# Layer 1's values and gates: where the stage's buffers lie, when its first loads go out, and the order of its tiles

## The chip, the core and the metric

The kernel runs on one core of one Trainium2 chip. A core has five engines that work from queues of their own: TensorE (PE in the profile; its weight loads are PEld), VectorE (DVE), ScalarE (ACT), GpSimd (POOL) and SyncE (SP), which here only issues DMAs. Each engine takes its instructions in a fixed order and waits on semaphores, so an instruction that waits holds up all that stand behind it on its engine. The metric is the device time of one execution in microseconds (us); less is better. SBUF is the on-chip memory with 128 partitions, PSUM the banks into which TensorE writes.

## The reference

Two layers over 2048 latent tokens and 256 context tokens of width 1024. The second, odd layer is the one that matters here. It multiplies the normalized tokens by one wide weight matrix and gets queries, keys, values and gates; queries and keys are normalized per head. Each token, on a grid of 32 rows by 64 columns, attends to a window of 8 by 16 neighbours with a bias per offset, and to all context tokens:

```python
q, k, v, z = jnp.split(u, 4, axis=-1)
...
s_lat = s_lat + bias.astype(jnp.float32)[None]
s_lat = jnp.where(col_mask[None, None, :, None, :], s_lat, -jnp.inf)
s_ctx = jnp.einsum('bqhd,bchd->bhqc', qr, k_ctx, preferred_element_type=jnp.float32) * scale
p = jax.nn.softmax(jnp.concatenate([s_lat, s_ctx], axis=-1), axis=-1)
...
y = jnp.dot(o.reshape(...) * jax.nn.silu(z_x), w_out)
x = x + gate * y
```

All is float32. The kernel makes a product of that precision from three matmuls: each operand is split into a high and a low part, and high x high, high x low and low x high are summed.

## The kernel before

Tokens come in 18 tiles of 128: tiles 0 and 1 are context, 2 to 17 latent. The odd layer's weights come in 8 groups of 512 columns, called j: 0 and 1 are queries, 2 and 3 keys, 4 and 5 values, 6 and 7 gates. A *cell* (t, j) is the product of tile t with group j: 8 steps of three 512-column matmuls. A gate cell takes two tiles at once and has 16 steps of six 256-column matmuls, in two halves with a PSUM bank each.

**`odd_qk`** makes queries and keys, and at its end also some of values and gates. Its last cells are, for tiles 16 and 17, groups 0 to 3, then the gate cell with group 6, then (16, 4) and (17, 4). Its pool `osA` holds, in the order of first use: the gains, two squares (2 KB per partition each), four small sums, four outputs `onat` (2 KB), two high and two low query tiles `oqh`, `oql` (2 KB) and four key tiles `okt` (8 KB). Key tiles, values and gates are stored to memory by DMAs that GpSimd issues (L1394, L1428, L1433).

**`odd_vz`** makes the rest of values and gates, and beside it, per head, each query's largest score (`maxes`), which attention needs. `weave` interleaves the two: after each step of a product come 0.57 steps of row maxima on average, and a product may run at most 15 steps of maxima ahead. One step of maxima is two matmuls, scores against the context keys (L1500) and against the window's keys (L1507). VectorE reduces them; for the window it adds the head's table first (L1513). The table is a bias (L1484, loaded) to which GpSimd adds two masks (L1485, L1486). ScalarE copies the head's queries into a half-zeroed tile `mz` (L106 from `by_tile`); VectorE zeroes the other halves once (L1467). Loads of the mask, queries, keys and tables are issued by SyncE, later queries by ScalarE.

A tile's cells need its high and low parts. There is room for two tiles; when a tile's last cell is done, `reload` brings the tile after next: load `x` (L376), ScalarE's copy to the high part, VectorE's subtraction for the low part (L380). A gate runs through ScalarE's tanh and VectorE's product (L1415) into a value buffer `ovz`; the bank comes free after that. There are two banks for products and six for the maxima.

The pools of `odd_vz` (`osB`, `omB`) lie over `osA`. A new tile waits for the last use of each old tile under it, among them DMAs that still store it.

**`odd_attention`** begins when the products end. Its loads are chained in one order on SyncE (`load`, L111). Its pools lie over the weights and pools of the stages before: query tiles, the first two tables and the first mask over the weights of groups 6 and 7, the key chunks over those of group 6. It starts with two steps against context keys, then takes window steps, whose scores get a masked table on VectorE (L1773); the products with the values follow some steps later (L1624, L1642).

The order of instructions on each engine is set by a planner that runs through the program with times of its own and gives each engine the instruction that is ready first, older ones ahead.

Of the kernel before, what the change touches and what calls it, by code (L numbers as in the profile page):

```python
# [17 lines left out]
P = 128  # L18
# [70 lines left out]
class Kern:  # L89
# [282 lines left out]
    def reload(self, l, t):  # L372

        nc, sp = self.nc, self.prp
        x = self.tl(sp, [P, D], "x", bufs=1)
        nc.sync.dma_start(x[:], self.H[l, t])  # L376
        h = x[:].rearrange("p (k t) -> p k t", k=KD)
        hi, lo = self.slots(t)
        self.act(hi, h)
        nc.vector.tensor_tensor(out=lo, in0=h, in1=hi, op=ALU.subtract)  # L380
        return hi, lo
# [910 lines left out]
    def odd_qk(self, ws, win, hT):  # L1292
# [7 lines left out]
        with ExitStack() as es:  # L1300
# [101 lines left out]
            for j in (0, 1, 2, 3, 6, 4):  # L1402
                cells += [((NT - 2, NT - 1), j)] if j == 6 else [(t, j) for t in (NT - 2, NT - 1)]
# [31 lines left out]
    def odd_vz(self, ws, win, hT):  # L1435
# [3 lines left out]
        with ExitStack() as es:  # L1439
            sp = self.pool(es, "osB", bufs=2, side="left", reuse_waits="tile")  # L1440
            mp = self.pool(es, "omB", bufs=2, side="left", reuse_waits="tile")
            pp = self.pool(es, "opB", bufs=2, space=PSUM, reuse_waits="tile")
            mk = self.tl(mp, [P, NR + NC], "maskq", bufs=1)
            nc.sync.dma_start(mk[:], self.i["maskq"])

            def cell(t, j):
                wh, wl = win[j]
                w = lambda k: wh[:, k, :], lambda k: wl[k][:]
                if j > 5:
                    for b in (0, 2):  # L1450
                        ps = self.tl(pp, [P, 512], "gm")
                        yield from self.pair_steps(ps, b, w)
                        n = self.tl(sp, [P, 512], "ovz", bufs=3)
                        self.gate(n, ps[:])
                        self.store_z(t, (j - 6) * 4 + b, n)
# [4 lines left out]
                n = self.tl(sp, [P, 512], "ovz", bufs=3)  # L1460
# [3 lines left out]
            zq = [[self.tl(mp, [P, 512], f"mz{i}{a}", F32R, bufs=1) for a in range(2)] for i in range(2)]  # L1464
            for i in range(2):
                for z in zq[i]:
                    nc.vector.memset(z[64 - i * 64 : 128 - i * 64].bitcast(F32), 0.0)  # L1467

            def queries(n, eng):
                h, g = divmod(n, 4)  # L1470
                b = (h % 2) * 64
                q = self.tl(mp, [P, 512], "mq", F32R, bufs=1)
# [3 lines left out]
            def maxes():  # L1476
                post, q = None, queries(0, nc.sync)
                for h in range(16):
                    j, b = h // 2, (h % 2) * 64
                    if b == 0:  # L1480
                        k = self.tl(mp, [P, T], "mk", F32R, bufs=2)
                        nc.sync.dma_start(k[:].bitcast(F32), self.K1[j])
                    tb = self.tl(mp, [P, NR, NC], "mtab", bufs=2)
                    nc.sync.dma_start(tb[:], self.i["rpb_q"][h].rearrange("p (r c) -> p r c", r=NR))  # L1484
                    nc.gpsimd.tensor_tensor(out=tb[:], in0=tb[:], in1=mk[:, :NR].unsqueeze(2).to_broadcast([P, NR, NC]), op=ALU.add)  # L1485
                    nc.gpsimd.tensor_tensor(out=tb[:], in0=tb[:], in1=mk[:, NR:].unsqueeze(1).to_broadcast([P, NR, NC]), op=ALU.add)  # L1486
                    m = self.tl(mp, [P, 16, 5], "mm")
                    nc.vector.memset(m[:], -3e38)
                    kl = k[:, CTX:].rearrange("d (r c) -> d r c", r=32)
                    for R in range(16):  # L1490
                        g, c = divmod(R, 4)
                        if c == 0:
                            zt = zq[h % 2][g % 2]
# [28 lines left out]
                    def post(h=h, mc=mc):  # L1522
                        pt = self.tl(pp, [P, 512], "mx", bufs=6)
                        nc.tensor.transpose(pt[:16, :P], mc[:], self.ident[:])
                        r = self.tl(mp, [P, P], "mr", F32R, bufs=1)
# [7 lines left out]
            cells = [((NT - 1, NT - 2), 7), (NT - 1, 5), (NT - 2, 5)]  # L1533
            for t in range(NT - 4, 0, -2):
                cells += [(t + 1, 4), (t + 1, 5), ((t, t + 1), 6), ((t, t + 1), 7), (t, 4), (t, 5)]
            cells += [(t, j) for j in (4, 5) for t in (1, 0)]
            gemms = self.stream(cells, hT, cell, lambda t: self.reload(1, t))
# [3 lines left out]
    def odd_attention(self, out, right, left, wout):  # L1541
# [4 lines left out]
        with ExitStack() as es:  # L1546
# [26 lines left out]
            for x in ones["kc"] + ones["kt"]:  # L1573
                nc.gpsimd.memset(x[64:65].bitcast(F32), 1.0)
# [12 lines left out]
            def values(j):  # L1587
                V = self.tl(vp[j % 2], [P, NT, P], "ov", bufs=1)
# [14 lines left out]
            def mask(tabs, mk):  # L1603
                for tb in tabs:
                    nc.gpsimd.tensor_tensor(out=tb[:], in0=tb[:], in1=mk, op=ALU.add)
# [95 lines left out]
            mask(tabs[0], load_mask(first.rearrange("p (r c) -> p r c", r=NR)))  # L1701
            kt.append(chunk(0, 0))
            V[0] = values(0)
            kt.append(chunk(0, 1))
            values_ctx(0, V[0])
# [241 lines left out]
```

## Time and profile before

| | us |
|---|---|
| median of 3 runs | 3570.43 |
| lowest, highest | 3565.54, 3573.92 |
| the profiled execution | 3572.7 |
| its span | 3570.9 |

| engine | busy us | share |
|---|---|---|
| TensorE matmul | 3492.2 | 98% |
| VectorE | 2384.3 | 67% |
| ScalarE | 1403.2 | 39% |
| GpSimd | 1221.3 | 34% |

The stage in question lies between about 2550 and 2995 us of the span; attention follows. A row of a timeline reads: start, length, engine, line, operation, out<-in, shape, count, and in brackets how long the engine stood idle before it and what ended that. A row of waits reads: who waited for whom, total us, times, longest. The chain is the work that ended last, followed back from the end. L106 and L111 are helpers that record many different instructions; there the tile's name tells which it is.

### The profile page before, as it was taken

The page shows a single profiled execution, that of the slowest core. Times are in us where ns is not written, and L with a number is a line of the kernel's source. Part 1 is how long each engine was busy: PE and PEld are TensorE (multiplying, and loading weights), DVE is VectorE, ACT ScalarE, POOL GpSimd, SP SyncE. Part 2 cuts the span into 40 slices and gives each one's busy share as a digit, 9 for nine tenths or more (in the row PEclk, how much of TensorE's full clock was granted, in tenths as well). Part 3 has the DMA queues.
Part 4 walks back from the last instruction along what each step waited for, and adds up shares of the span by engine and source line. Part 5 has one row for each costly group of instructions (what it writes and reads, how often), then busy time and mean ns, then how long its engine had stood idle before and what let it go on. Part 6 is the DMA issues. An engine that isn't in the chain of part 4 may idle for free.

```text
span 3570.9 us, 53484 instructions
## 1 busy us (share of the span) xinstructions
PE 3492.2 (98%) x19260; PEld 2758.9 (77%) x19260; DVE 2384.3 (67%) x5020; ACT 1403.2 (39%) x2656; POOL 1221.3 (34%) x1363
## 2 busy tenths in 40 slices
PE   8999999999999999999999999999999999999899
PEld 6888999999996666665667878888798997555577
DVE  4677767888886777798764344544688883777721
ACT  4545551111116555555553124444422223555510
POOL 1443430101011222212312233333454544777744
PEclk9999999999999999999999999999999999999999
DMA  7555554222243343424534554556744338887654
GB/s 254 150 148 168 146 173 125 87 77 87 68 120 86 81 110 83 108 76 125 155 112 145 162 168 122 148 150 174 227 149 153 118 125 222 218 216 212 181 179 148
DMA packets 386914, 513.75 MB, mean 144 GB/s; under 512 B 61229, under 2 KB 264061, under 8 KB 380746
## 3 DMA queue, kind: packets, MB, share of 16 engines
q1 hardware_dynamic: 353242, 418.68, 40.4%
q0 software_dynamic: 21888, 62.56, 5.9%
q10 hardware_dynamic: 11520, 29.09, 2.4%
q8 instruction: 153, 2.51, 0.3%
q14 instruction: 111, 0.91, 0.1%
HBM read 330.61 MB, written 179.59 MB: 143 GB/s over the span
## 4 chain that ended last, share of the span: by engine, by line
PE 85%; DVE 6%; DMA 4%; ACT 2%; issue 2%; POOL 2%; SPq 0%; POOLq 0%; DVEq 0%; ACTq 0%
PE gm L131 8%; PE gm L129 8%; PE gm L130 8%; PE av L1008 6%; PE mx L707 4%; PE st L1066 4%; PE st L1067 3%; PE st L1068 3%; PE gm L190 3%; PE gm L191 3%; PE gm L192 3%; PE o L1642 2%; PE st L1612 2%; PE st L129 2%; PE o L1624 2%; PE st L130 2%
## 5 line engine op out<-in xcount | busy, mean ns | idle before, releaser
L1057 DVE TENSOR_TENSOR acc<-acc,apt 128x512 f32<-128x512 f32 x512 | 380.7, 775 | 141.9 <-ACT apt L106 139.2
L708 DVE TENSOR_REDUCE mm<-mx 128x1 f32<-128x512 f32 (+1 forms) x656 | 391.0, 628 | 86.2 <-PE mx L707 78.9
L106 ACT ACTIVATE apt<-st 128x512 f32<-128x512 f32 (+1 forms) x592 | 345.5, 595 | 243.8 <-PE st L1068 204.6
L1008 PE MATMUL av<-apt,av 128*64 128x512 f32 (+1 forms) x1184 | 270.0, 592 | 0.0
L1066 PE MATMUL st<-aq,akh 97*128 97x512 f32 x576 | 245.5, 426 | 0.6 <-ACT apt L106 0.2
L707 PE MATMUL mx<-mk,mq 96*128 96x512 f32 (+1 forms) x656 | 241.7, 371 | 0.0
L106 ACT ACTIVATE u<-gm 128x352 f32<-128x352 f32 (+1 forms) x144 | 70.5, 497 | 428.4 <-PE gm L131 182.6
L1067 PE MATMUL st<-aq,akh 96*128 96x512 f32 x576 | 228.1, 396 | 0.0
L1068 PE MATMUL st<-aq,akl 96*128 96x512 f32 x576 | 227.9, 396 | 0.0
L106 ACT ACTIVATE opt<-opt 128x930 f32<-128x930 f32 (+9 forms) x144 | 119.5, 830 | 231.7 <-POOL opt L1813 139.6
L1513 DVE CUSTOM_DVE_ANT_1 mx<-mx,mtab 128x465 f32<-128x465 f32 (+12 forms) x576 | 180.1, 342 | 31.4 <-PE mx L1507 25.9
L1008 PEld LDWEIGHTS av<-apt,av 128*64 128x64 f32 x1184 | 80.1, 136 | 152.7 <-issue 150.1
L1773 DVE TENSOR_TENSOR opt<-st,tab 128x64 f32<-128x64 f32 (+10 forms) x576 | 142.9, 314 | 72.3 <-PE st L1613 39.3
L1648 POOL TENSOR_TENSOR oacc<-oacc,opt 128x682 f32<-128x682 f32 (+9 forms) x144 | 173.2, 1224 | 31.9 <-ACT opt L106 30.6
L1066 PEld LDWEIGHTS st<-aq,akh 97*128 97x128 f32 x576 | 108.3, 188 | 72.5 <-issue 42.1
L1068 PEld LDWEIGHTS st<-aq,akl 96*128 96x128 f32 x576 | 109.5, 190 | 25.2
L707 PEld LDWEIGHTS mx<-mk,mq 96*128 96x128 f32 x656 | 123.3, 188 | 6.0
L1067 PEld LDWEIGHTS st<-aq,akh 96*128 96x128 f32 x576 | 109.9, 191 | 16.9
L106 ACT ACTIVATE x<-px,modB,modA 128x128 f32<-128x128 f32 x272 | 99.3, 469 | 59.3 <-PE px L355 49.6
L131 PE MATMUL gm<-w0h,hlo 128*128 128x512 f32 x288 | 114.1, 396 | 5.4 <-DVE hlo L380 5.4
L1612 PE MATMUL st<-q,kt 128*128 128x480 f32 (+5 forms) x256 | 98.8, 388 | 20.4 <-DVE opt L1773 15.3
L129 PE MATMUL gm<-w1h,hhi 128*128 128x512 f32 x288 | 115.1, 400 | 2.9 <-DVE ovz L1415 2.9
(594 smaller groups left out, 10288.1 us busy)
## 6 DMA issues: line engine op xcount, KB each, us to landing
q<-Q SPq DMA_DIRECT2D x48, 512.0 KB
H<-x ACTq DMA_DIRECT2D x36, 512.0 KB
adaw<-ada_w SPq DMA_DIRECT2D x64, 256.0 KB
x<-H SPq DMA_DIRECT2D x32, 512.0 KB
K1t<-okt POOLq DMA_DIRECT2D x32, 512.0 KB, 6.8
kt<-K1t SPq DMA_DIRECT2D x32, 512.0 KB
mtab<-rpb_q SPq DMA_DIRECT2D x16, 899.0 KB
QT<-qkhl SPq DMA_DIRECT2D x36, 384.0 KB
```

The source lines that it names most:

```text
L106: return self.nc.scalar.activation(out, in_, func, **kw)
L129: self.nc.tensor.matmul(out, lh(k), rh(k), start=j == 0, stop=False)
L130: self.nc.tensor.matmul(out, lh(k), rl(k), start=False, stop=False)
L131: yield self.nc.tensor.matmul(out, ll(k), rh(k), start=False, stop=j == n - 1)
L707: mm = nc.tensor.matmul(ps[:, :w], q[:A_QK, (t % 6) * P : (t % 6) * P + P], k[:A_QK, k0 : k0 + w], start=True, stop=True)
L708: nc.vector.tensor_reduce(out=m[:, t, n : n + 1], in_=ps[:, :w], axis=AX.X, op=ALU.max)
L1008: nc.tensor.matmul(O[j, nb][i * 64 : i * 64 + 64, :w], V[j, kt // TT][:, kt % TT, i * 64 : i * 64 + 64], pts[i][:, :w], start=n == 0, stop ...
L1057: self.add = nc.vector.tensor_tensor(out=acc[i][:, :w], in0=a[:, :w], in1=pts[i][:, :w], op=ALU.add)
L1066: nc.tensor.matmul(ps[:, :w], kh[: A_QK + 1, i, kq], qh[: A_QK + 1, :w], start=True, stop=False)
L1067: nc.tensor.matmul(ps[:, :w], kh[:A_QK, i, kq], ql[:A_QK, :w], start=False, stop=False)
L1068: mm = nc.tensor.matmul(ps[:, :w], kl[:A_QK, i, kq], qh[:A_QK, :w], start=False, stop=True)
L1513: nc.vector.tensor_tensor_reduce(out=s, in0=s, in1=tb[:, ri : ri + rn, ci : ci + cn], scale=1.0, scalar=-3e38, op0=ALU.add, op1=ALU.max, a ...
```

## The change

The diff has six parts.

- The cell (16, 4) moves from the end of `odd_qk` into `odd_vz`, after (16, 5).
- `osB` and `omB` become one pool. Its tiles are asked for in a written order, with two gaps, so that each lies over particular tiles of `osA`: queries and two zeroed tiles first, then the other two zeroed tiles, the value buffers, the first keys, the first table, the mask, the second table, the second keys.
- The first two tables are loaded and masked, and the first keys loaded, at the head of the stage's program (`table`, `ready`, `held`). The first two gate stores are put behind the last of these four additions on GpSimd.
- The load of tile 15's `x` becomes a function of its own (`fetch_x`) called at the head of the stage.
- The context tiles' four cells come third (after tiles 14 and 15), and the stage ends with the cells of tiles 2 and 3 in a new order: values of group 4, both gate cells, values of group 5.
- In attention, the ones in the key tiles and the mask additions of the first two tables go from GpSimd to VectorE, and the first values are loaded after the context's values and the second key chunk, not before.

```diff
-                cells += [((NT - 2, NT - 1), j)] if j == 6 else [(t, j) for t in (NT - 2, NT - 1)]
+                cells += [((NT - 2, NT - 1), j)] if j == 6 else [(t, j) for t in (NT - 2, NT - 1) if j != 4 or t == NT - 1]
...
-            sp = self.pool(es, "osB", bufs=2, side="left", reuse_waits="tile")
-            mp = self.pool(es, "omB", bufs=2, side="left", reuse_waits="tile")
+            sp = mp = self.pool(es, "omB", bufs=2, side="left", reuse_waits="tile")
...
+            begun = {NT - 3: self.fetch_x(1, NT - 3)}
...
+            first = [query()]
+            zq = {(0, 0): zero(0, 0), (1, 0): zero(1, 0)}
+            gap(0, 40)
+            zq[0, 1], zq[1, 1] = zero(0, 1), zero(1, 1)
+            rows = [row()]
+            gap(1, 384)
+            free = [wide()]
+            held = [keys(0)]
+            tabs_of = [tabs(0)]
+            highs = [high()]
             mk = self.tl(mp, [P, NR + NC], "maskq", bufs=1)
+            tabs_of.append(tabs(1))
+            held.append(keys(1))
             nc.sync.dma_start(mk[:], self.i["maskq"])
+
+            def table(h):
+                tb = tabs_of.pop(0) if tabs_of else tabs(h % 2)
+                nc.sync.dma_start(tb[:], self.i["rpb_q"][h].rearrange("p (r c) -> p r c", r=NR))
+                nc.gpsimd.tensor_tensor(out=tb[:], in0=tb[:], in1=mk[:, :NR].unsqueeze(2).to_broadcast([P, NR, NC]), op=ALU.add)
+                self.added = nc.gpsimd.tensor_tensor(out=tb[:], in0=tb[:], in1=mk[:, NR:].unsqueeze(1).to_broadcast([P, NR, NC]), op=ALU.add)
+                return tb
+
+            ready = [table(0)]
+            nc.sync.dma_start(held[0][:].bitcast(F32), self.K1[0])
+            ready.append(table(1))
+            stop = [self.added] * 2
...
-                        self.store_z(t, (j - 6) * 4 + b, n)
+                        with self.tc.issue_after(stop.pop().ins) if stop else ExitStack():
+                            self.store_z(t, (j - 6) * 4 + b, n)
...
-            cells = [((NT - 1, NT - 2), 7), (NT - 1, 5), (NT - 2, 5)]
-            for t in range(NT - 4, 0, -2):
+            cells = [((NT - 1, NT - 2), 7), (NT - 1, 5), (NT - 2, 5), (NT - 2, 4)]
+            for t in range(NT - 4, 2, -2):
                 cells += [(t + 1, 4), (t + 1, 5), ((t, t + 1), 6), ((t, t + 1), 7), (t, 4), (t, 5)]
-            cells += [(t, j) for j in (4, 5) for t in (1, 0)]
+                if t == NT - 4:
+                    cells += [(x, j) for x in (1, 0) for j in (4, 5)]
+            cells += [(3, 4), (2, 4), ((2, 3), 6), ((2, 3), 7), (3, 5), (2, 5)]
...
             for x in ones["kc"] + ones["kt"]:
-                nc.gpsimd.memset(x[64:65].bitcast(F32), 1.0)
+                nc.vector.memset(x[64:65].bitcast(F32), 1.0)
...
-            mask(tabs[0], load_mask(first.rearrange("p (r c) -> p r c", r=NR)))
+            mask(tabs[0], load_mask(first.rearrange("p (r c) -> p r c", r=NR)), nc.vector)
             kt.append(chunk(0, 0))
-            V[0] = values(0)
+            V[0] = self.tl(vp[0], [P, NT, P], "ov", bufs=1)
+            values_ctx(0, V[0])
             kt.append(chunk(0, 1))
-            values_ctx(0, V[0])
+            values(0, V[0])
```

57 lines of the change are left out of this document (32 added, 25 removed).

## The prediction

> **What bounds the kernel now.** I read the page first, then the stage in which layer 1's values and gates are made (2540 to 3000 us) by windows, then TensorE's waits there, the chain, and last the single queues.
>
> ```profile
> span 3570.9 us, 53484 instructions
> PE 3492.2 (98%) x19260; PEld 2758.9 (77%) x19260; DVE 2384.3 (67%) x5020; ACT 1403.2 (39%) x2656; POOL 1221.3 (34%) x1363
> ```
>
> TensorE is busy for 98% of the span, so only its gaps and its slow matmuls can be won. The windows (time, then busy us of PE, PEld, DVE, ACT, POOL, granted clock, DMA share, GB/s) show where they lie:
>
> ```profile
> 2550.00:2560.00 10.00, 10.00 (x87) 9.89 (x86) 1.06 (x3) 0.60 (x1) 1.05 (x2) 1.00 0.44 133
> 2560.00:2570.00 10.00, 6.68 (x33) 5.71 (x32) 3.64 (x8) 1.71 (x3) 2.48 (x2) 0.83 0.94 328
> 2570.00:2580.00 10.00, 9.56 (x43) 7.66 (x42) 5.89 (x1) 2.69 (x4) 9.99 (x6) 1.00 0.48 187
> 2580.00:2590.00 10.00, 5.09 (x15) 4.07 (x16) 7.67 (x17) 1.55 (x2) 3.75 (x2) 0.66 0.28 91
> ```
>
> ```profile
> 2980.00:2990.00 10.00, 10.00 (x45) 8.22 (x44) 0.00 (x0) 0.83 (x2) 4.81 (x2) 1.00 1.11 344
> 2990.00:3000.00 10.00, 10.00 (x44) 7.39 (x43) 2.03 (x4) 4.69 (x10) 0.00 (x0) 1.00 0.69 192
> ```
>
> Only the stage's start (first fence) has holes; its end (second), where attention takes over, has none. TensorE's waits of the stage, by releaser (total, times, longest):
>
> ```profile
> PE gm L131 <- DVE hlo L380: 5.4, 1, 5.4
> PE gm L129 <- DVE ovz L1415: 2.9, 1, 2.9
> ...
> PE mx L1500 <- DMA mk<-K: 0.5, 1, 0.5
> ```
>
> The second of these stands ahead of tile 17's first product with weights 5:
>
> ```profile
> 2564.41 0.56 PE L129 MATMUL gm<-w1h,hhi 128*128 128x512 f32 x1 [2.85 <-DVE ovz L1415]
> ```
>
> And the chain through the two holes (start, length):
>
> ```profile
> 2552.10 6.28 DMA V<-onat
> 2558.73 0.49 DVE mz L1467
> ...
> 2568.39 0.23 PE gm L129
> ...
> 2574.11 10.76 DVE hlo L380
> 2584.91 0.80 PE gm L131
> 2585.71 0.43 PE gm L129
> ...
> 2588.27 0.43 PE gm L129
> ```
>
> **Hole one** is 2.9 + 0.5 us of waiting, and the matmuls behind it run at half pace (0.43 us for 512 columns, as behind hole two at 2585.71, where 0.23 is usual, as at 2568.39). The granted clock of 0.83 over 2560 to 2570 prices that: 10 x 0.17 = 1.7 us. Together 5.1 us.
>
> **Hole two** is 5.4 us, and behind it one piece of 0.80 and seven of 0.43 (2585.71 to 2588.27) instead of 0.23: 0.6 + 7 x 0.20 = 2.0. Together 7.4 us. Both holes: **12.5 us**, 0.35% of the time; the windows show no other in the stage's start, so this is about the most that can be won.
>
> Why hole two: VectorE's subtraction for token tile 15 took 10.76 us, and these stand beside it on VectorE and GpSimd:
>
> ```profile
> 2572.16 3.22 POOL L1485 TENSOR_TENSOR mtab<-mtab,maskq 128x1798 f32<-128x1798 f32 x1
> 2575.33 3.71 POOL L1486 TENSOR_TENSOR mtab<-mtab,maskq 128x1798 f32<-128x1798 f32 x1
> ...
> 2580.10 3.67 POOL L1486 TENSOR_TENSOR mtab<-mtab,maskq 128x1798 f32<-128x1798 f32 x1
> ```
>
> ```profile
> 2589.34 1.23 DVE L380 TENSOR_TENSOR hlo<-x,hhi 128x1024 fp32r<-128x1024 f32 x1 [2.33 <-ACT hhi L106]
> ```
>
> The next such subtraction takes 1.23 us. The long one began inside GpSimd's table additions and ended 1.1 us after the last of them: it stood still for 9.5 us.
>
> Why hole one: the new pools lie over tiles still being stored. SyncE's and ScalarE's rows, and the stores (KB each, median us to landing):
>
> ```profile
> 2558.52 0.34 SPq L1444 DMA_DIRECT2D maskq<-maskq  x1
> ```
>
> ```profile
> 2562.52 0.63 ACT L106 ACTIVATE mz<-mq 64x512 fp32r<-64x512 f32 x1 [11.24 <-DMA mq<-Q]
> ```
>
> ```profile
> K1t<-okt POOLq DMA_DIRECT2D x4, 512.0 KB, 9.4
> V<-onat POOLq DMA_DIRECT2D x4, 128.0 KB, 8.8
> z<-onat POOLq DMA_DIRECT2D x1, 256.0 KB, 13.5
> ```
>
> All loads of the stage queue behind the mask's at 2558.52. ScalarE waited 11.24 us for the first queries with the first gate's tanh behind it, so VectorE's product came late and the score bank with it.
>
> **The change part by part.**
>
> *The moved cell.* (16, 4), 24 matmuls of 0.23 us = 5.5 us, goes from the stage before to after (16, 5). TensorE's sum is the same. Between tile 17's last product and tile 15's first there are now two cells, 11 us, and not one. The subtraction may still meet the additions of the second table; at its longest (10.76 us plus 1.1 us for the copy ahead of it) it now fits into 11 us plus some row maxima. Hole two goes: **-7.4 us**, bounds -7.4 and, if the collision outlasts the cover by a few us, -4.
>
> *Buffers.* By tile sizes in order of first use, the old pool is: gains, two squares, four 2 KB outputs, two high and two low query tiles, four 8 KB key tiles. The new single pool puts the first queries and two zeroed tiles on gains, squares and the first output; zeroed tiles three and four on outputs two and three; the value buffers on the high and a low query tile; the first keys on a low query tile and key tile one; the first table on key tiles one and two; the second on two and three. So keys and first table wait only for the first four key stores:
>
> ```profile
> 2532.97 2.55 POOL L1394 DMA_DIRECT2D K1t<-okt  x4
> ```
>
> With a landing of about 9.4 us that is 2542 to 2545, in place of 2558.5. The queries wait for the last use of the gains, about 2542. Moved ahead by some 13 us are: mask, two tables, keys, queries, and GpSimd's four additions (3.2 + 3.7 us each pair). Behind SyncE's early waits stands nothing else but these loads.
>
> What is late next: VectorE's zeroing of tiles three and four needs a gate store and the value store of (17, 4), which lands at 2558.4 now (2552.10 + 6.28). The cells of tiles 16 and 17 run 5.5 us earlier than now: hole one opens at 2564.4 - 2.9 = 2561.5, so (17, 5) wants its bank at 2556, and the gate that must leave it is half a gate cell (5.5 us) older, ready at about 2551. If the zeroing is issued first, VectorE holds that bank until about 2559: 3 us of waiting and some 1.7 of slow matmuls, hole one as it is today. If not, hole one goes. Bounds: -5.1 and, with the loads slowing the stores (rival one), +7. I take **-1**, near the row that is there today, because the queries at least come off the path.
>
> *Gate stores held behind the additions.* Two stores move from about 2552 to the end of the second table's additions, some 2568. Behind them waits only the reuse of the value buffers, by (16, 5), which ends after 2567. **0**, bounds 0 and +3.
>
> *First tile's load on its own.* Its load is issued early already,
>
> ```profile
> 2488.44 0.33 SPq L376 DMA_DIRECT2D x<-H  x1
> ```
>
> 70 us before the stage: 0. Bounds -0.5 and 0.5.
>
> *Context tiles third.* Same cells, same cover of 11 us at every change of tile: 0 on TensorE. At the end the last cells become (3, 5) and (2, 5), and gate group 7, whose last product ScalarE takes up here,
>
> ```profile
> 2962.30 0.60 ACT L106 ACTIVATE ovz<-gm 128x512 f32<-128x512 f32 x1 [4.78 <-PE gm L192]
> ```
>
> ends 11 us before the stage's last product, not 33:
>
> ```profile
> 2995.26 0.60 ACT L106 ACTIVATE ovz<-gm 128x512 f32<-128x512 f32 x1 [4.89 <-PE gm L131]
> ```
>
> Attention's second query tile, first tables and first mask lie over group 7's weights, so their loads move to 11 us before the end. Against that, keys and the first queries load earlier. In group 7's shadow stand 0.5 MB of queries, 1.6 MB of tables and mask, 0.8 of keys, 0.1 context values, 0.8 keys, 1.0 values. First needs now:
>
> ```profile
> 2999.97 1.20 DVE opt L1773 x8
> ```
>
> for tables and keys, and for the values
>
> ```profile
> 3007.03 0.49 PE o L1642 x8
> ```
>
> that is 4.7 and 11.8 us after the stage's end, or 15.7 and 22.8 after group 7. At 280 GB/s, between the windows' 192 and 344, the first 2.1 MB take 7.5 us, 2 us for landing, 2.5 us of masking: 12. All 4.9 MB and 0.8 MB of stores take 20.4 + 2 = 22.4. Both fit, barely: **+0.5**, bounds 0 and +10.
>
> *Masks and ones on VectorE.*
>
> ```profile
> 2983.24 4.81 POOL L1605 TENSOR_TENSOR tab<-tab,q 128x1034 f32<-128x1034 f32 x2 [7.30 <-DMA q<-maskk]
> ```
>
> On VectorE the masks take about 2 x 1.23 us (the 1024-wide row above), 2.3 us less, in a window where it is idle (0.00 busy in 2980:2990). Already counted; otherwise 0. Behind the waiting mask stands attention's first sum, not needed before.
>
> **Sum.** -7.4 - 1 + 0.5 = -8 us. The profiled run took 3572.7 us (span 3570.9 and 1.8 around it), 2.3 above the median of 3570.4; I take it from the median: **3562.5 us**.
>
> **Rivals.**
>
> One, *the first hole grows* (about 3570). Loads of 2.3 MB now run in 2542 to 2557, where the DMA engines store key tiles: at the 328 GB/s of 2560:2570, 7 us of their time. If the value store lands that much later, at 2565, the zeroing holds the gate's bank until 2566: 10 us and 2 of slow matmuls, +7 on hole one, and the gain of hole two is eaten: net 0. For it: the 13.5 us of the gate store under load. Against: only if the zeroing stands ahead on VectorE. [...]
>
> Two, *slower: attention starts hungry* (about 3579). If the loads behind group 7 run at 150 GB/s, as the 133 of 2550:2560 shows possible, 5.7 MB take 38 + 2 us, the first values come 17 us late, and the net is +9. It decides below about 160 GB/s. Against it: 344 in 2980:2990.
>
> Three, *the change doesn't do what it says* (about 3566): SyncE still issues the mask first and the queries last; hole one stays, hole two shrinks by half.
>
> **How the numbers follow.** Forecast 0.54 (0.46 of it beyond 0.2%), rival one 0.24 (0.03 slower), rival two 0.17, rival three 0.05 (0.01 faster). Bound of what can be told: 0.2%, 7.1 us. Faster 0.47, same 0.33, slower 0.20. The likeliest case alone spans 3558 (both holes gone) to 3566; with rivals one, three and the milder half of two, 3557 to 3575.
>
> **What would show it.** Right: no TensorE wait on the subtraction near 2580, all four additions done before it or under cover, first keys landed before 2556. Wrong: a wait on the value product (L1415's) of over 5 us near 2556, VectorE idle there on a store of values; in attention, TensorE waiting on tables or values within 15 us of its start. What would make it wrong above all is the order on VectorE between zeroing and first gate.

## The result, and the profile after

The changed kernel takes 3582.42 us (median of 8 runs, 3579.48 to 3584.93), the one before 3572.18 in the runs beside it. The ratio is 1.0028, interval 1.0019 to 1.0037: **10 us slower**, where 3562.5 with 3557 to 3575 had been forecast. The profiled execution took 3584.3 us.

First the page of the changed kernel, then its windows in the columns known from before (time, length, busy us of PE, PEld, DVE, ACT and POOL, granted clock, DMA share, GB/s):

```profile
span 3582.5 us, 53484 instructions
PE 3498.1 (98%) x19260; PEld 2761.8 (77%) x19260; DVE 2382.0 (66%) x5026; ACT 1402.1 (39%) x2656; POOL 1217.7 (34%) x1357
```

```profile
2550.00:2560.00 10.00, 7.38 (x66) 7.18 (x64) 0.00 (x0) 1.19 (x2) 0.00 (x0) 1.00 1.01 327
2560.00:2570.00 10.00, 2.63 (x6) 2.14 (x7) 1.80 (x5) 0.63 (x1) 9.69 (x3) 0.62 0.72 267
2570.00:2580.00 10.00, 10.00 (x43) 8.21 (x43) 1.83 (x4) 2.06 (x3) 3.08 (x4) 0.87 0.16 30
...
2990.00:3000.00 10.00, 9.31 (x40) 7.01 (x38) 0.00 (x0) 1.38 (x3) 2.13 (x4) 1.00 1.03 346
3000.00:3010.00 10.00, 7.10 (x27) 4.99 (x28) 8.58 (x28) 5.92 (x11) 1.79 (x2) 0.81 1.12 287
```

Two holes show: one at 2557 to 2567, far larger than any before, and one in attention's first 12 us, where before had none. TensorE's waits name what ended them:

```profile
PE gm L129 <- DVE ovz L1420: 10.0, 1, 10.0
PE st L1648 <- DVE opt L1810: 2.3, 1, 2.3
```

No wait on the subtraction (now L385) is left; it takes 1.23 us where it took 10.76. **Hole two is gone, hole one has more than doubled.** VectorE's timeline shows why:

```profile
2548.05 1.12 DVE L1503 MEMSET mz<- 64x512 f32 x2 [0.40 <-DMA z<-onat]
2566.11 0.48 DVE L1503 MEMSET mz<- 64x512 f32 x1 [16.94 <-DMA V<-onat]
2566.70 1.21 DVE L1420 SCALAR_TENSOR_TENSOR ovz<-ovz,gm 128x512 f32<-128x512 f32 x2
...
2576.48 1.23 DVE L385 TENSOR_TENSOR hlo<-x,hhi 128x1024 fp32r<-128x1024 f32 x1 [8.57 <-ACT hhi L106]
```

The zeroing of the fourth query tile waits 16.94 us for a store of values, and both gate products stand behind it. ScalarE had done the first gate's tanh already:

```profile
2552.03 0.60 ACT L106 ACTIVATE ovz<-gm 128x512 f32<-128x512 f32 x1 [4.92 <-PE gm L192]
```

In the chain that store is the piece ahead of the hole:

```profile
2547.95 17.95 DMA V<-onat
...
2566.77 0.56 DVE ovz L1420
2567.37 0.79 PE gm L129
2568.16 0.43 PE gm L130
```

Before, the store took 6.28 us and landed at 2558.4; now it is issued 4 us earlier, takes 17.95 and lands at 2565.9. Beside it SyncE issues the stage's loads, which before waited until 2558.5:

```profile
2546.26 0.34 SPq L1469 DMA_DIRECT2D maskq<-maskq  x1
2546.71 2.31 SPq L1473 DMA_DIRECT2D mtab<-rpb_q  x1
2549.18 1.49 SPq L1479 DMA_DIRECT2D mk<-K  x1
2554.90 0.33 SPq L1473 DMA_DIRECT2D mtab<-rpb_q  x1
```

At attention's start the second queries wait for group 7's weights, and the masks stand on VectorE behind the first context sums, though VectorE was idle ahead of both:

```profile
2974.91 11.63 SPq L111 DMA_DIRECT2D q<-Q  x3
```

```profile
3001.42 1.29 DVE L1668 TENSOR_TENSOR wo<-opt 128x512 f32<-128x512 f32 x2 [12.69 <-ACT opt L106]
3002.63 2.38 DVE L1641 TENSOR_TENSOR tab<-tab,q 128x1034 f32<-128x1034 f32 x2
...
3006.13 4.36 DVE L1810 TENSOR_TENSOR opt<-st,tab 128x32 f32<-128x32 f32 x24
```

Where the 11.6 us between the two spans lie (attention begins with its first score matmul; its first 40 matmuls run from there to the start of the 41st):

| | before | after | difference |
|---|---|---|---|
| ahead of the stage: issue of the last four key stores | 2541.4 | 2542.7 | +1.3 |
| hole one: wait, and matmuls at half pace | 5.1 | 10.0 + 2.7 | +7.6 |
| hole two | 7.4 | 0 | -7.4 |
| the stage: from that issue to attention's start | 453.7 | 455.2 | +1.5 |
| attention to the end of the span | 575.8 | 584.6 | +8.8 |
| of it its first 40 matmuls | 10.1 | 15.0 | +4.9 |

The first row hardly hangs on the edits: over all kernels below that issue falls anywhere from 2537.5 to 2544.2. So the stage's length, 453.7 and 455.2 us here, is what they are compared by. All lengths of stages here come from one profiled execution of each kernel. Of attention's 8.8 us, 4.9 come at its start; most of the rest are two more stretches of 3.4 us at half the clock later on, 1.7 us lost in each. The clock varies from run to run: the runs of the kernel before have mean clocks of 0.989 to 0.994, and 0.001 of 3570 us is 3.6 us. Whether the later stretches are chance alone is not shown: over the nine profiles of kernels with the context tiles third, attention loses between -0.5 and 5.9 us behind its first 40 matmuls, against the kernel before.

### The profile page after: what moved, and what is told of

Its sections match the earlier page's. It is cut to its first block, busy times and chain, and to the rows that moved or that the text cites. A ratio compares the mean times of both kernels' runs of the same rounds, so it can differ in the third digit from the quotient of the medians.

```text
span 3582.5 us, 53484 instructions
## 1 busy us (share of the span) xinstructions
PE 3498.1 (98%) x19260; PEld 2761.8 (77%) x19260; DVE 2382.0 (66%) x5026; ACT 1402.1 (39%) x2656; POOL 1217.7 (34%) x1357
## 5 line engine op out<-in xcount | busy, mean ns | idle before, releaser
L1547 DVE CUSTOM_DVE_ANT_1 mx<-mx,mtab 128x217 f32<-128x217 f32 (+13 forms) x576 | 180.4, 342 | 34.3 <-PE mx L1541 25.8
L129 PE MATMUL gm<-w0h,hhi 128*128 128x512 f32 x288 | 114.7, 398 | 2.4 <-DVE hhi L367 2.4
```

Source lines behind the costliest of these rows:

```text
L129: self.nc.tensor.matmul(out, lh(k), rh(k), start=j == 0, stop=False)
L1547: nc.vector.tensor_tensor_reduce(out=s, in0=s, in1=tb[:, ri : ri + rn, ci : ci + cn], scale=1.0, scalar=-3e38, op0=ALU.add, op1=ALU.max, a ...
```

## The experiments

Each run's time is a median, each ratio is to the kernel before, from runs on the same chip. The kernel before took 3572.2 to 3573.9 us beside them; a comparison with the changed kernel goes across these groups of runs.

### Hole one: the zeroed tile

One zeroing, of the tile that lies over the late store's source, moves to its first use and behind the gate's product:

```diff
...
-            for (i, _), z in zq.items():
-                nc.vector.memset(z[64 - i * 64 : 128 - i * 64].bitcast(F32), 0.0)
+            for (i, a), z in zq.items():
+                if (i, a) != (1, 1):
+                    nc.vector.memset(z[64 - i * 64 : 128 - i * 64].bitcast(F32), 0.0)
...
                             zt = zq[h % 2, g % 2]
+                            if (h, g) == (1, 1):
+                                with self.tc.issue_after(self.last_gate.ins):
+                                    nc.vector.memset(zt[:64].bitcast(F32), 0.0)
```

> The changed kernel, only the zeroing of the fourth half-zeroed tile is put behind the second gate's product on VectorE. Theory Z (VectorE stands in that zeroing until the value store of (17, 4) lands, and so holds the first gate's bank): the TensorE wait of 10.0 us on L1420 near 2557 goes, with about 2.7 us of matmuls at half pace behind it; 12 us less than the changed kernel, about 3570. Rival L (the early loads and the stores starve the stage, whatever VectorE does): TensorE stops a few us later for the first queries, which land at 2567 in the changed kernel; 0 to 5 us less, 3577 to 3582.

Measured: 3572.08 us, ratio 0.9998 (0.9988 to 1.0008), 10 us under the changed kernel. VectorE and then TensorE's longest wait in this stage:

```profile
2548.36 0.69 DVE L1420 SCALAR_TENSOR_TENSOR ovz<-ovz,gm 128x512 f32<-128x512 f32 x1 [3.48 <-ACT ovz L106]
2553.76 0.69 DVE L1420 SCALAR_TENSOR_TENSOR ovz<-ovz,gm 128x512 f32<-128x512 f32 x1 [4.71 <-ACT ovz L106]
2562.80 0.48 DVE L1531 MEMSET mz<- 64x512 f32 x1 [8.36 <-DMA V<-onat]
```

```profile
PE mx L1538 <- ACT mz L106: 3.0, 1, 3.0
```

The store is as late as ever, but both gates are done long before it. The wait of 10.0 us is gone, 3.0 us remain before the first maxima, and the stage takes 447.2 us, 8.0 less. So the place of one memset on VectorE costs the changed kernel 8 us in the stage, most of the 10 by which it is slower. That does not say yet why the store is late.

### Hole one: the loads beside the store

In the first attempt the loads move back in the program to where they stood before:

```diff
-            ready = [table(0)]
-            nc.sync.dma_start(held[0][:].bitcast(F32), self.K1[0])
-            ready.append(table(1))
-            stop = [self.added] * 2
+            ready, stop = [], []
...
-                        if j:
-                            nc.sync.dma_start(k[:].bitcast(F32), self.K1[j])
+                        nc.sync.dma_start(k[:].bitcast(F32), self.K1[j])
```

> The changed kernel with one thing undone: the first tables and the first keys are loaded where the kernel before loads them, at the head of the maxima, and the last gate's stores no longer wait for the table's second sum; buffers, cells and attention stay as changed. It asks why the value store of tile 17 landed at 2565.9, 18.5 us after it was issued. Theory L (rival one of the prediction: the loads run among the stores and take their share of the DMA): without them the store lands within 6 to 8 us of its issue, near 2554, the zeroing and the gate follow, the first hole falls from 12.7 us to 4 to 6 and the kernel is 6 to 8 us faster in the stage, unless the maxima then wait for tables or keys (a wait of up to 5 us before the first maximum). Theory S (the stores themselves stand in line, eight key stores, z and V within 13 us): the store still lands after 2562, the hole stays over 9 us and the time at 3578 to 3585.

Measured: 3579.63 us, ratio 1.0015 (1.0005 to 1.0025); a wait of 10.2 us. SyncE's rows show that it settles nothing on the loads:

```profile
2547.08 1.41 SPq L1515 DMA_DIRECT2D mk<-K  x1
2548.55 4.25 SPq L1473 DMA_DIRECT2D mtab<-rpb_q  x2
```

They go out when their buffers come free, wherever the program has them: the written order is not what makes them early. So the second attempt makes SyncE wait, by a load of what the store writes:

```diff
+            stored = self.V1[0].rearrange("(q a) d -> a q d", a=8)[7, 192:256, :8]
+            nc.sync.dma_start(self.tl(mp, [64, 8], "seen", bufs=1)[:], stored)
             nc.sync.dma_start(mk[:], self.i["maskq"])
```

> The changed kernel with one small load put ahead of the stage's first loads on SyncE's queue: it reads 64 rows of the values that tile 17 has just stored, so SyncE waits until that store has landed, as it did before the change (there the first table of masks waited for it by its place in the buffers). Nothing else differs, and the data that it reads are not used. In the last run but three the loads had moved in the program but not in time (they still went out from 2545 on), so that run told nothing of them. Theory L (rival one: loads beside the stores starve them): the second value store of tile 17, issued at about 2547.5, lands near 2559 instead of 2565.9, the zeroing and the gate follow at 2559 to 2560, the wait before the next cell falls from 10.0 us to 2.5 to 4, and the stage is 5 to 8 us shorter unless the maxima then wait for their loads (up to 3 us). Theory S (the stores hold each other up): the store lands after 2563 as before, and the hole keeps 8 us or more.

Measured: 3576.84 us, ratio 1.0014 (1.0005 to 1.0023), 5.6 us under the changed kernel; the stage takes 448.3 us, 6.9 less. GpSimd's issue of the store, VectorE's zeroing that waits for it, and TensorE's wait:

```profile
2548.94 1.07 POOL L1433 DMA_DIRECT2D V<-onat  x2 [1.54 <-ACT onat L106]
```

```profile
2560.37 0.48 DVE L1505 MEMSET mz<- 64x512 f32 x1 [9.47 <-DMA V<-onat]
```

```profile
PE gm L129 <- DVE ovz L1420: 2.7, 1, 2.7
```

With the loads held back the store lands some 11 us after its issue, not 18, and TensorE waits 2.7 us, not 10.0. **The loads beside it cost the store about 7 us**, and that is what more than doubled hole one. (The intervals of this ratio and the changed kernel's just overlap; the conclusion rests on the store and the wait.) The 11 us are still more than the 6.28 before, but the store is issued earlier now: counted from the issue of the last four key stores it lands after 17.0 us before the change, 16.0 here and 23.2 in the changed kernel. Its earlier issue hardly brought its landing forward.

### Each part alone

The moved cell on the kernel before:

```diff
-                cells += [((NT - 2, NT - 1), j)] if j == 6 else [(t, j) for t in (NT - 2, NT - 1)]
+                cells += [((NT - 2, NT - 1), j)] if j == 6 else [(t, j) for t in (NT - 2, NT - 1) if j != 4 or t == NT - 1]
...
-            cells = [((NT - 1, NT - 2), 7), (NT - 1, 5), (NT - 2, 5)]
+            cells = [((NT - 1, NT - 2), 7), (NT - 1, 5), (NT - 2, 5), (NT - 2, 4)]
```

> The kernel before with the one cell (16, 4) moved behind (16, 5), nothing else. Theory P of the prediction (hole two is VectorE's subtraction held by GpSimd's additions, with one cell of cover): TensorE's 5.4 us on L380 go with 2.0 us of half pace, hole one stays: 7 us less than before, about 3565. Rival: GpSimd's additions run as late as now, the subtraction is held as long, and the first row maxima wait for the masked table instead: 0 to 3 us less.

Measured: 3574.14 us, ratio 1.0000 (0.9988 to 1.0011). The wait on the subtraction is gone, and the other has grown from 2.9 us:

```profile
PE gm L129 <- DVE ovz L1415: 8.7, 1, 8.7
```

```profile
2557.86 1.03 DVE L1467 MEMSET mz<- 64x512 f32 x2 [16.08 <-DMA V<-onat]
```

The gates come a cell (5.5 us) earlier, the zeroing ahead of them does not. With the cell gone from `odd_qk` the old buffers come free earlier too: the mask's load waits for a store of gates and no longer for the last one of values, so it goes out at 2542.64, not 2558.52, and the first keys follow,

```profile
2545.24 2.37 SPq L1482 DMA_DIRECT2D mk<-K  x1
```

and the store beside them takes 14.9 us, where it took 6.28. So the new buffers are not needed to bring the loads into the store's time. What hole two gave, hole one takes: the stage is 453.2 us long, for 453.7.

The context tiles' new place on the kernel before:

```diff
-            for t in range(NT - 4, 0, -2):
+            for t in range(NT - 4, 2, -2):
                 cells += [(t + 1, 4), (t + 1, 5), ((t, t + 1), 6), ((t, t + 1), 7), (t, 4), (t, 5)]
-            cells += [(t, j) for j in (4, 5) for t in (1, 0)]
+                if t == NT - 4:
+                    cells += [(x, j) for x in (1, 0) for j in (4, 5)]
+            cells += [(3, 4), (2, 4), ((2, 3), 6), ((2, 3), 7), (3, 5), (2, 5)]
```

> The kernel before with the context tiles third and the new end of the stage, nothing else. Theory G: attention starts late by 5 to 9 us, 3577 to 3581, TensorE waiting in its first 15 us on VectorE's additions of tables. Rival M (it is the masks on VectorE that cost): no more than 2 us slower than before, since the masks stay on GpSimd.

Measured: 3574.57 us, ratio 1.0003 (0.9992 to 1.0014), in two parts that cancel: with the new plan there is no wait on the subtraction and the stage takes 448.7 us, 5.0 less; attention's first 40 matmuls take 12.9 us for 10.1, and attention is 6.8 us longer. The masks run here at 2990.45, where before they were over at 2988.05, and what they wait for is the load of the mask, which now comes behind group 7's weights. Theory G's late start is there, if smaller than it said; the time is not, because of what the stage wins:

```profile
2990.45 4.79 POOL L1607 TENSOR_TENSOR tab<-tab,q 128x1034 f32<-128x1034 f32 x2 [2.59 <-DMA q<-maskk]
```

Next the old cell order on the changed kernel (the last diff backwards), and then the buffers with the first loads and gate stores alone (the moved cell and attention's edits undone as well):

> The changed kernel with the cells of tiles 14 to 0 in the old order, context tiles last; all else as changed. Theory G (attention's second query tile, first tables and first mask wait for the weights of gate group 7, which now end 11 us before attention and not 33): TensorE's first 40 matmuls of attention lose the 4.9 us they lose more than before, and VectorE's masks are done before attention's first sums; 5 to 8 us less than the changed kernel, about 3576. Rival M (the masks on VectorE stand behind attention's first sums, whatever the loads do): the gap before L1810's first addition stays, 0 to 2 us less.

> The changed kernel with all undone but the buffers and the first loads: the values' cell of tile 16 back ahead of the stage, the context cells last, attention's masks, ones and order of loads as before. Theory Z with L (the zeroed tile over the source of a late store, and loads beside the stores): the store of tile 16's values is issued some 5 us later than the one of tile 17 and lands at 2562 to 2567, the first hole is 5 to 9 us where it was 5.1 before, the second stays at 5 to 7, and attention starts late as in the run with the old order of cells on these buffers (a wait of up to 8 us for the first queries, whose buffers now lie over the last stores): 3580 to 3592. If the buffers cost nothing by themselves, as the prediction had it, the time is 3570 to 3574.

Measured: 3593.96 us (ratio 1.0057, 1.0039 to 1.0076) and 3594.35 us (1.0055, 1.0040 to 1.0069): both 11 to 12 us **slower** than the changed kernel. The first expectation had the wrong sign. TensorE's waits of the second run, SyncE's in attention's start, and the windows there:

```profile
PE st L1646 <- DMA q<-Q: 8.5, 1, 8.5
PE gm L129 <- DVE ovz L1420: 8.0, 1, 8.0
```

```profile
SPq L111 <- DMA V1c<-ovz: 26.6, 4, 11.5
```

```profile
2990.00:3000.00 10.00, 5.77 (x26) 4.39 (x24) 0.00 (x0) 1.20 (x2) 0.00 (x0) 1.00 0.47 111
3000.00:3010.00 10.00, 5.50 (x12) 3.73 (x13) 0.74 (x2) 2.35 (x5) 0.00 (x0) 0.52 0.96 278
3010.00:3020.00 10.00, 7.51 (x21) 5.32 (x21) 8.87 (x19) 2.61 (x6) 5.17 (x2) 0.50 1.14 257
```

On the new buffers attention's first queries and keys lie over the value buffers `ovz`, and with the context cells last SyncE waits 26.6 us for their stores. Behind that wait the granted clock is 0.52 and 0.50 in the two windows from 3000 to 3020, and 0.79 in the next: halved for some 24 us. So the buffers, with the loads that go with them, cost 20 us: a little in hole one (8.0 us of waiting for 2.9), most at attention's start. Hole two is gone here too, with the cell where it was, since the table additions come earlier. The context tiles third, which cost attention 6.8 us on the old buffers, win 11 to 12 in all on the new ones: the stage's last stores are then others, and SyncE waits for none of them there. The parts don't add up: 0, 0 and +20 alone, +10 together. Attention's edits were not run alone.

### Attention's start: the masks' place

Masks back on GpSimd, the rest as changed:

```diff
-            mask(tabs[0], load_mask(first.rearrange("p (r c) -> p r c", r=NR)), nc.vector)
+            mask(tabs[0], load_mask(first.rearrange("p (r c) -> p r c", r=NR)))
```

> The changed kernel with one thing undone: attention's first masks go back from VectorE to GpSimd; its ones and the order of its loads stay as changed. In the changed kernel the masks (2.38 us at 3002.63) stood on VectorE behind the first context sums, and the table sums of the first block began at 3006.13. Theory A (the masks' place on VectorE is most of the late start): attention's first 40 matmuls fall from 15.0 us to about 11, GpSimd masks at about 2993 to 2998, and the kernel is 3 to 5 us faster than the changed one (about 3578). Theory B (the late loads cost it, whoever masks: the first queries wait 11.63 us for group 7's weights): GpSimd's masks take 4.8 us where VectorE's took 2.4 and end no earlier, the first 40 matmuls stay at 14 to 16 us and the time at 3580 to 3584. The first hole of the stage (about 12.7 us) is the same under both.

Measured: 3579.08 us, ratio 1.0018 (1.0009 to 1.0028); the first 40 matmuls take 14.5 us for 15.0, the stage 453.2 for 455.2. The start is as late as Theory B had it; the time lies 3 us under the changed kernel's, but the two intervals overlap. GpSimd:

```profile
2996.74 1.04 POOL L1433 DMA_DIRECT2D V<-ovz  x2 [4.40 <-ACT ovz L106]
2997.80 4.78 POOL L1641 TENSOR_TENSOR tab<-tab,q 128x1034 f32<-128x1034 f32 x2
```

The masks stand behind the issue of the last values' stores, which wait for the stage's last cell. Before the change the last stores were those of the context's values, and ScalarE issues these (L1424): GpSimd was free.

Then all of attention's edits undone, with the zeroing moved as above (masks and ones on GpSimd, `values(0)` ahead of `values_ctx(0, V[0])`); and the same with the gates of tiles 2 and 3 ahead of their values:

```diff
-            cells += [(3, 4), (2, 4), ((2, 3), 6), ((2, 3), 7), (3, 5), (2, 5)]
+            cells += [((2, 3), 6), ((2, 3), 7), (3, 4), (2, 4), (3, 5), (2, 5)]
```

> The changed kernel with the zeroing of the fourth query tile moved behind the gate (as in the run that took the first hole away) and with all of attention's own edits undone: masks and ones on GpSimd, the values loaded ahead of the context values. The order of the cells stays as changed (context third). If attention's edits cost the 6 us that it still lost there, the time falls from 3572 to about 3566 and attention's length from 582.1 to about 576. If it is the order of the cells (group 7's weights held to the end, so that the first queries come late), attention keeps 580 to 583 us and the time stays at 3570 to 3573.

> The run before this one (fourth zeroing behind the gate, attention's own edits undone) with the last six cells in another order: the gates of tiles 2 and 3 (groups 6 and 7) ahead of their values, so that group 7's weights end two cells, about 11 us, earlier. Theory B (late loads): the first queries' loads go out about 11 us earlier, attention's first 40 matmuls take about 10 us, and the time is 3 to 5 us under that of the run before, at 3562 to 3566; it would then beat both kernels. If the late start comes from elsewhere, nothing changes (3568 to 3572). Risk: tiles 2 and 3 must both be reloaded and split a cell earlier, and a wait of 2 to 5 us on the split of tile 2 or 3 would show some 33 us before the stage's end.

In the second, tile 2 comes into the place of tile 4 while that is still needed, so tile 4's values are computed from tile 2; the amount of work is the same. Measured: 3574.51 us (1.0006, 0.9995 to 1.0017) and 3578.06 (1.0012, 1.0001 to 1.0024). Undoing attention's edits wins nothing. Nor do earlier loads: in the second run the mask's load goes out at 2969.91 (2980.13 in the first), and the first 40 matmuls take 16.7 us (15.1):

```profile
2991.11 1.04 POOL L1433 DMA_DIRECT2D V<-ovz  x2 [4.50 <-ACT ovz L106]
2992.14 0.98 POOL L1614 MEMSET kc<- 1x512 f32 x2
2993.21 4.75 POOL L1645 TENSOR_TENSOR tab<-tab,q 128x1034 f32<-128x1034 f32 x2
```

It is GpSimd's queue again, as far as its rows tell. So what is late at the start is the masks: with the old buffers for their load, here for the place that they have in an engine's queue. The last run of this group gives them a better one, with the zeroing moved too:

```diff
...
                 for i, a in enumerate(sums(acc, n)):
-                    nc.vector.tensor_tensor(out=a, in0=pts[i][:, 0, :], in1=pts[i][:, 1, :], op=ALU.add)
+                    with self.tc.issue_after(masked.ins):
+                        nc.vector.tensor_tensor(out=a, in0=pts[i][:, 0, :], in1=pts[i][:, 1, :], op=ALU.add)
```

> The changed kernel with the fourth zeroing behind the gate (3572 us) and attention's first masks still on VectorE but ahead of the first context sums there, where the queue has been idle for 12.7 us. If the masks' place behind the sums is what attention's start waits for, the masks run at about 2984 to 2988 (loads allowing), the wait of 2.3 us before the first scores of the second block goes, the first 40 matmuls take 10.5 to 12 us for 13.8, and the time is 2 to 5 us under that run: 3567 to 3570. If the loads are what is late, the masks wait for the mask's load, the context sums stand behind them, and the time stays within 2 us of it or gets worse.

Measured: 3569.86 us, ratio 0.9995 (0.9986 to 1.0003). VectorE, then TensorE further on:

```profile
2985.57 2.38 DVE L1645 TENSOR_TENSOR tab<-tab,q 128x1034 f32<-128x1034 f32 x2 [7.27 <-DMA q<-maskk]
2991.48 2.65 DVE L1674 TENSOR_TENSOR wo<-opt 128x512 f32<-128x512 f32 x4 [3.52 <-ACT opt L106]
```

```profile
3024.01 0.36 PE L1653 MATMUL st<-q,kt 128*128 128x264 f32 x1 [2.41 <-DMA kt<-K1t]
```

The masks start before attention's first score (2987.45), as soon as their load has landed; the wait of 2.3 us goes, and the first 40 matmuls take 11.2 us for 13.8. That the masks' place delayed the start is shown. That it is worth time is not: this profile loses the gain again at 3024 on a late key chunk, and the intervals of the two versions (0.9998 and 0.9995) overlap. Why that chunk is late stays open.

### A version that beats both

The kernel before with the cell moved, the zeroing behind the first gates and the first copy of queries behind their tanh; the maxima start 16 steps later and then run slightly faster; old buffers, old cell order at the end, old attention:

```diff
...
                         self.store_z(t, (j - 6) * 4 + b, n)
+                    while blank:
+                        with self.tc.issue_after(self.last_gate.ins):
+                            nc.vector.memset(blank.pop(0).bitcast(F32), 0.0)
                     return
...
-                            self.by_tile(zt[b : b + 64], q[b : b + 64])
+                            with self.tc.issue_after(self.last_tanh.ins) if h + g == 0 else ExitStack():
+                                self.by_tile(zt[b : b + 64], q[b : b + 64])
...
-            self.weave(gemms, maxes(), 0.57, 15)
+            self.weave(gemms, maxes(), 0.59, 15, head=16)
```

> The kernel before with two edits: the values' cell of tile 16 moved behind the first gates (as in the run of that cell alone, 3574 us), and the zeroing of the query tiles and the first copy of queries moved behind the first gates on their engines (the maxima start 16 steps later and run at 0.59 for 0.57 so that they end where they did). Buffers, cell order at the end and attention are the ones of before. If the hole of 8.7 us that the moved cell opened there is only the zeroing's wait for a store, it goes, attention keeps its 566 to 567 us from its first score, and the time is 8 to 11 us under that run: 3562 to 3566, better than both kernels. If the maxima, now later, become the end of the stage (the first queries of attention wait for them), part of it comes back: 3567 to 3572.

Measured: **3564.66 us, ratio 0.9975 (0.9964 to 0.9986)**: 9 us under the kernel before, 18 under the changed one. TensorE's one wait in the stage, and VectorE:

```profile
PE gm L129 <- DVE ovz L1415: 2.3, 1, 2.3
```

```profile
2557.25 0.22 DVE L1489 MEMSET mm<- 128x80 f32 x2 [11.91 <-DMA K1t<-okt]
2557.38 1.22 DVE L1415 SCALAR_TENSOR_TENSOR ovz<-ovz,gm 128x512 f32<-128x512 f32 x2
2561.38 1.02 DVE L1458 MEMSET mz<- 64x512 f32 x2 [2.79 <-DMA V<-onat]
```

The gates leave their banks some 3 us before the store lands, the first 40 matmuls of attention take 9.6 us, and the stage takes 444.3 us for 453.7. The 2.3 us that are left have a cause of the same kind: another memset, of the tile that collects the maxima, stands ahead of the gates on VectorE and waits for a store of keys. So the prediction's -8 us was there to be had, from one cell, the places of five instructions and the later start of the maxima. The cell alone had won nothing; the other two were not run apart.

## Why the prediction was wrong

- **Hole two** (forecast -7.4): right in its size. No wait on the subtraction remains in the changed kernel, nor with the cell moved alone. But the cover of 11 us was not put to the test: in the changed kernel the subtraction fell between two additions of GpSimd and took 1.23 us, with the cell alone it met one and took 2.42, not 10.76. And the cell was not the only way to it: the wait is gone with the buffers alone and with the new cell order alone too.
- **Buffers** (taken as -1, bounds -5.1 and +7): this step failed first. Hole one went from 5.1 to 12.7 us, +7.6, past the upper bound. Rival one described the event almost to the microsecond: store landed at 2565 (2565.9), bank held to 2566 (2566.7), 10 us of wait (10.0). It got a chance of 0.24 and a price of 7 us, and the sum took -1 "because the queries at least come off the path". That they did was of no use: the zeroing stood in the same path. The text named the order on VectorE as what would decide, and left that order undecided. The step that failed inside it is the landing time: it took the store's 2558.4 from the old trace, though its own working had just moved the loads into the stores' time. The loads beside it made that 2565.9. That rival one hit so closely is in part luck: its 2.3 MB leave out the second table (0.9 MB), which went out at 2554.90, while the store was still moving. And the term belongs to the moved cell as much as to the buffers: the cell alone brings the loads forward and makes hole one's wait 8.7 us.
- The same step looked only at the stage's start. Which old tile lies under which new one also decides when attention's first loads go out, and with the old cell order this costs 8.5 us of waiting (buffers alone: +20 us in all). The prediction saw neither that nor that the new cell order takes most of it away.
- **Context tiles third** (+0.5, bounds 0 and +10): attention is 8.8 us longer, inside the bounds, but far from the value taken. Rival two expected first values 17 us late, from loads at under 160 GB/s. The rate was 346 GB/s in 2990:3000, and loads 10 us earlier did not help. The 2 us that the step counted for a landing are what a store of 2 KB took before (`M<-mr`, median of 64: 2.0 us); for attention's loads no row shows one. At the start what is late is the masks; why attention stays 7 us longer with the masks first (582.9 us, for 575.8) is open.
- **Masks on VectorE** (0): the step said that they run "in a window where it is idle". VectorE was idle, for 12.69 us, and the masks still ran after it, because the planner put them behind two context sums. With the masks first, the first 40 matmuls take 2.6 us less (13.8 to 11.2).
- **Gate stores** (0) and the **first tile's load** (0): the runs show nothing against either; neither was tried alone (the run with the loads moved in the program also lets the gate stores go, and its stage is 455.6 us long, for 455.2).
- **The sum**: -7.4 + 7.6 + 8.8 + 2.6 (the rest of the stage and ahead of it) = 11.6 in the profile, 10 in the medians, for -8. The rivals were priced as if one excluded the other. They lie in different stages: rival one came in whole, and in the place of rival two there was a late start too, though not by its mechanism. No case of the prediction had a loss in both stages. Both signs that it had named for being wrong in these places were there: VectorE idle on a store of values, and TensorE waiting for the tables' additions within 15 us of attention's start.

## What to carry to other kernels

Before a buffer is put where it comes free earlier, list what its first writers wait for and what stands behind each of them on its engine: one 0.48 us memset over the source of a slow store cost 8 to 10 us, and moving the memset was worth more than the whole new layout. Here the loads that started earlier put the landing of the store beside them off by about 7 us (18 us after its issue, 11 with the loads held back), and the landing time read from the old trace didn't hold: ask what will be moving beside a transfer. VectorE was idle for 12.69 us ahead of two context sums, and the masks still ran behind them: look up the instruction's place in its queue. And where two risks lie in different stages, add them.

## What the runs showed of the hardware

One wait of TensorE cost about twice its length. In the run of the buffers alone it waited 8.5 us for queries, until 3004.24, and in the three windows from 3000 to 3030 the granted clock was 0.52, 0.50 (both shown above) and

```profile
3020.00:3030.00 10.00, 10.00 (x49) 5.62 (x48) 2.94 (x14) 4.10 (x8) 6.27 (x4) 0.79 1.04 230
```

That is 10 x (0.48 + 0.50 + 0.21) = 11.9 us of clock. The clock records of before and after have two rates, 1.00 and 0.50. With these the 0.52 of the first window means that the half clock began at about 3000.4, so some 2 us of the loss fall into the wait itself; and in the second window TensorE stood idle for 2.5 us. By this estimate some 9 us were lost behind a wait of 8.5 us, and the half clock lasted 11.9 / 0.5, some 24 us. The half-clock stretches in the records of before and after are shorter: 3.4 or 6.8 us, once 10.2 (after, hole one), and the one that ends with the program 8.1 and 8.4 us. Why the clock stayed low for some 20 us after TensorE had taken up work again (busy for 5.50 and 7.51 us of two windows) is not settled by these runs.

The same two stores of 128 KB landed 6 us (before), 11 us (loads held back) and 18 us (changed) after the issue. The first was issued 5 us later behind the key stores than the other two; the last had loads beside it, of which 4.6 MB moved in the 30 us around it:

```profile
q0 software_dynamic: 1166, 4.06, 48.2%
q1 hardware_dynamic: 1328, 4.64, 40.7%
```

These are the DMA queues of the changed kernel in 2540 to 2570 (packets, MB, share of 16 engines): stores from GpSimd in the first row, SyncE's loads in the second.

VectorE's subtraction for a token tile (two inputs of 1024 columns) took 1.22 to 1.24 us in the profiles of before and after, from 2500 us on, where no table addition of GpSimd ran beside it. It began while an addition was running seven times. Six times it ended 1.1 us after the end of that addition, having taken 1.22, 3.13 and 3.75 us (before) and 3.54, 2.60 and 2.22 us (after); in hole two it ended 1.1 us after the last of three, having taken 10.76 us. Of three subtractions into which an addition fell after 0.8 to 1.1 us, two ended 1.1 us behind that addition (5.94 us before, 5.67 after) and one took 1.23 us. By these times it made next to no headway beside an addition that was running when it began.
